# Hybrid decoder block on one core: the first stage with z's first two products in it, norms issued ahead, and other rooms up to the x stage

## The chip, the cores and the metric

The kernel runs on one core of one Trainium2 chip. The metric is the device time of one execution in microseconds; the median of three runs is given. Everything is float32 outside the matmuls; a float32 product is made of three matmuls of rounded parts (high x high, high x low, low x high).

## The reference

One decoder layer over x of 1024 tokens by 1024. Only its first lines matter here:

```python
h = rms_norm(x, g_pre_mix[l])
q, k, v, z, xbc, dt_raw, ga, gs = _split(h @ w_in[l], IN_SIZES)
o_att = stick_breaking_attention(q, k, v)          # heads split and joined
o_ssm = ssd_branch(z, xbc, dt_raw, ...)            # uses silu(z)
merged = sigmoid(ga) * (o_att @ w_br_att[l]) + sigmoid(gs) * (o_ssm @ w_br_ssm[l])
x = x + rms_norm(merged @ w_mix_out[l], g_post_mix[l])
...                                                # cross-attention, SwiGLU
```

q, k and v are 1024 wide each, z 2048, x|B|C 3072, dt 32, the two gates 1024 each.

## The kernel before

The work is a list of instructions for five engines (TensorE, VectorE or DVE, ScalarE or ACT, GpSimd or POOL, and SyncE or SP, whose one queue issues every transfer). Python code writes them in one order. A scheduler then places them by a model of their times: each engine takes, of what the model finds ready, what the code wrote first. On the chip every engine, and SP's queue, runs its own list strictly in order, and waits are semaphores. Memory is cut into pools; a pool is opened and closed with the code block that owns it, on the left or the right end of each partition's memory, and a tile waits for the readers of what lay in its place.

**Strassen-Winograd.** The wide projections of h are made as 2 x 2 block products with seven products in place of eight. h transposed is cut into quarters: b11 and b21 (features 0 to 511 and 512 to 1023 of tokens 0 to 511) and b12, b22 (the same of tokens 512 to 1023), and the combinations t1 = b12 - b11, t2 = b22 - t1, t3 = b22 - b12, t4 = b21 - t2. Each is kept as a rounded part and a residue (`b11h`, `b11l`, ...).

**First stage (the first `with ExitStack() as p1`, pools from `t4x0` on).** `load_x` brings 128 tokens into a tile. `normed(c)` squares it on ACT with a running sum (L332), takes 1/sqrt on POOL (`rstd_of`, L163 and L164) and scales on DVE (L333). `turned` transposes it on TensorE, four 128 x 128 blocks to a PSUM bank (L339). `put` writes rounded part (ACT, L344) and residue (L345). `first_half(c)` for c = 0 to 3 does this for b11 and b21 and also copies both whole to the tiles x11 and x21 (ACT, L365). `second_half(c)` does b12 (rounded by L93, residue by L96 on POOL, both stored to `hb_d`), b22, and the four combinations, t1 from x11 (L380) and t4 from x21 (L384). `dt_raw` makes the 32 columns of dt, 24 small matmuls for each group of tokens (L99 to L101). v's first two products, `a11` x b11 and `a12` x b21, run beside this: `product` gives four steps; a step rounds a 128 x 512 piece of weights (`zh`, ACT, L93), takes its residue (`zl`, DVE, L96) and makes 12 matmuls of 128 x 512 (L287 to L289) into four PSUM banks.

**Second stage (pools `zraw2`, `zk`, `zo`, `zw2`).** `token_major(j, ...)` does a 1024-column block of v (j = 0) or z (j = 1, 2). Its weight blocks b11_, b21_, b22_, b12_ are 1 MB each, in two tiles `zr` of four (`zraw`) and six (`zraw2`) rooms. Products in order: b11 (with a copy u of it), t2, b21, t1, t3, b22, t4, the first and third already done for j = 0. The sums of weights s1, s3, s2 (L468, L470, L472; DVE for j = 0, else POOL) and s4 (L480, POOL) come between. `put_v` and `put_z` (sigmoid on ACT, L432, product on DVE, L433) evacuate and store (L439, L434).

**x stage.** `winograd_weights` loads two tiles `wr` (L191), makes four sums `sf` on POOL (L194 to L197) and rounds seven weights into `sw`; `winograd_pair` runs the seven products (L218 to L220). Conv and gates follow, then attention, the state-space mixer, the output projections, cross-attention and the feed-forward, which uses `winograd_weights` too.

Of the kernel before, what the change touches and what calls it, by code (L numbers as in the profile page):

```python
# [8 lines left out]
F32 = mybir.dt.float32  # L9
# [25 lines left out]
def hybrid_block(ctx, tc, a, out, dbg=None):  # L35
# [20 lines left out]
    def scr(name, shape, dt=F32):  # L56
        return dram.tile(shape, dt, tag=name, name=name)
# [20 lines left out]
    x2_d = scr("x2_d", [S, D])  # L78
    x3_d = scr("x3_d", [S, D])


# [40 lines left out]

    def columns(pp, tag):

        with tc.tile_pool(name="prm", bufs=1) as prp:
            prm = [mk(prp, [P, P], F32, f"prm{i}") for i in range(2)]
            for t in prm:
                G.memset(t, 0.0)
            nc.sync.dma_start(prm[0][0:96, :], a["conv_w"][0].rearrange("t (f p) -> (t f) p", p=P))
            for nm, n in (("conv_b", 24), ("g_ssm_norm", 16)):  # L130
                nc.sync.dma_start(prm[1][rows[nm]:rows[nm] + n, :], a[nm][0].rearrange("(f p) -> f p", p=P))
            for i, t in enumerate(prm):
                ps = mk(pp, [P, 4, P], F32, tag)[:, 0]
                T.transpose(ps, t, ident)
                A.activation(prmT[:, i * P:(i + 1) * P], ps, AF.Copy)
        nc.sync.dma_start(dsk, a["d_skip"][0].partition_broadcast(P))
# [48 lines left out]
    def winograd_weights(rawp, sfp, swp, loads, pool_ops=0):  # L185

        r0 = mk(rawp, [P, 4, 2, P], F32, "wr")
        r1 = mk(rawp, [P, 4, 2, P], F32, "wr")
        for r, kh in ((r0, 0), (r1, 1)):
            for dst, s in loads(r, kh):  # L190
                nc.sync.dma_start(dst, s)  # L191
# [57 lines left out]
    with ExitStack() as pa:  # L249
# [51 lines left out]
        with ExitStack() as p1:  # L301
            t4 = pool(p1, "t4x0", 4)
            sv = pool(p1, "xsv")
            tt = pool(p1, "tcomb", 6)
            bt = pool(p1, "b12t", 1)
            mp = pool(p1, "memp")
# [4 lines left out]
            def load_x(c):  # L311
                xts[c] = mk(t4, [P, D], F32, "x4")
                nc.sync.dma_start(xts[c], x_in[c * P:(c + 1) * P, :])

            load_x(0)
            gx = load_gain(mp, "g_pre_mix")
            load_x(1)
# [7 lines left out]

            x11, x21 = [mk(sv, [P, 4, HALF], F32, n) for n in ("x11", "x21")]

            def normed(c):
                xt = xts[c]
                junk = mk(tt, [P, D], BF16, "tc")  # L330
                ms = mk(stats, [P, 1], F32, "ms")
                A.activation(junk, xt, AF.Square, scale=D ** -0.5, accum_out=ms)  # L332
                V.scalar_tensor_tensor(xt, xt, rstd_of(ms), gx, ALU.mult, ALU.mult)  # L333
                return xt

# [22 lines left out]
            def first_half(c):  # L358
                cs = slice(c * P, (c + 1) * P)
                y = normed(c)  # L360
                q = []
                for kh, (nm, whole_) in enumerate((("b11", x11), ("b21", x21))):
                    pt = turned(y, kh)
                    q.append(put(nm, c, pt))
                    A.activation(whole_[:, :, cs], pt, AF.Copy)  # L365
                return lambda: dt_raw(c, q)

            def second_half(c):

                cs = slice(c * P, (c + 1) * P)  # L370
                y = normed(c + 4)
                x12, x22 = turned(y, 0), turned(y, 1)
# [8 lines left out]
                V.tensor_tensor(t3, x22, t3, ALU.subtract)  # L381
                q22 = put("b22", c, x22)
                V.tensor_tensor(t2, x22, t1, ALU.subtract)
                V.tensor_tensor(t4_, x21[:, :, cs], t2, ALU.subtract)  # L384
                put("t2", c, t2, V)
                put("t1", c, t1, G)
# [4 lines left out]
            a11, a12 = None, None  # L391
            dts_ = []
            for c in range(4):
                dts_.append(first_half(c))
                if c == 0:
                    a11 = block(rv, 0, C_V)
                load_x(c + 4)
                if c == 1:
                    columns(psp, "tr")
                    a12 = block(rv, 512, C_V)  # L400
                if c > 0:
                    dts_.pop(0)()
            pa0 = [mk(psa, [P, HALF], F32, "ma") for _ in range(4)]
            steps = product(pa0, a11, "b11", True, False) + product(pa0, a12, "b21", False, True)
            for c in range(4):
                dts_.append(second_half(c))
                for _ in range(2):
                    steps.pop(0)()
                dts_.pop(0)()
                if c == 1:  # L410
                    u0 = copied(pa0)
            dts_.pop(0)()


        with ExitStack() as p1:
            rp = pool(p1, "zraw2", 6)
            kp = pool(p1, "zk", 6)
            op = pool(p1, "zo", 2)
            wps.append(pool(p1, "zw2", 3))
# [20 lines left out]

            def token_major(j, c0, put, i0):
                bb = ((psa, "ma"), (psb, "mb"))[::1 if j % 2 == 0 else -1]
# [18 lines left out]
                if j == 0:  # L461
                    pa_, u = pa0, u0
                else:
                    pa_ = bank(0)
                    times(pa_, b11_, "b11", True, False)
                s1 = [mk(rp, [P, 2, HALF], F32, "zr") for _ in range(2)]
                E_ = V if j == 0 else G
# [4 lines left out]
                both(lambda q: E_.tensor_tensor(s2[q], s1[q], b11_[q], ALU.subtract))  # L472
                if j > 0:
                    u = copied(pa_)
                pb_ = bank(1)
                times(pb_, s2, "t2", True, True)
                if j > 0:
                    times(pa_, b12_, "b21", False, True)
# [5 lines left out]
                times(pb_, s1, "t1", True, False)  # L484
                for c in range(4):
                    put(c, i0, pa_[c])
                pa_ = bank(0)
# [17 lines left out]

            token_major(0, C_V, put_v, 0)
            token_major(1, C_Z, put_z, 0)
            token_major(2, C_Z + 2 * HALF, put_z, 2)
# [964 lines left out]
    with ExitStack() as q4:  # L1473
        sfp = pool(q4, "fsf", 4, side="right")
        swp = pool(q4, "fsw", 7, side="right")
# [285 lines left out]
```

## Time and profile before

| | |
|---|---|
| median of 3 runs | 2646.32 us (2643.34 to 2647.19) |
| profiled execution | span 2654.0 us |
| TensorE matmul busy | 2519.6 us, 95% of the span |
| DVE busy | 1827.7 us, 69% |
| ACT busy | 1158.9 us, 44% |
| POOL busy | 874.8 us, 33% |
| HBM read, written | 192.37 MB, 68.82 MB |

The profiled execution is one run of its own, and its span is what the rows of the trace add up to; the runs are timed without the profiler. A busy TensorE is not TensorE at its peak, since its clock is gated. A line such as `tr<-ident,x` reads: tile tr is written, from tiles ident and x. In brackets stands how long the engine had been idle before, and what released it.

### The profile page before, as it was taken

How to read it: one execution, taken by the hardware profiler on the slowest of the kernel's cores; microseconds unless marked ns; L12 is line 12 of the kernel's file. 1: busy time of each engine (PE TensorE's matmuls, PEld its weight loads, DVE VectorE, ACT ScalarE, POOL GpSimd, SP SyncE). 2: the span in 40 equal slices, each digit the busy share in tenths (PEclk: the TensorE clock that was granted, in tenths of full speed). 3: DMA queues.
4: the chain of work that ended last, by engine and by line, in shares of the span. 5: the costliest groups of instructions: out<-in, count | busy, mean ns of one | idle time of the engine just before them, and what ended most of it. 6: DMA issues, size and time to landing. Idle time of an engine off the chain costs nothing. (4 is left out here: it accounts for less than half of the span.)

```text
span 2654.0 us, 32762 instructions
## 1 busy us (share of the span) xinstructions
PE 2519.6 (95%) x12090; PEld 2085.9 (79%) x12090; DVE 1827.7 (69%) x2118; ACT 1158.9 (44%) x2061; POOL 874.8 (33%) x684
## 2 busy tenths in 40 slices
PE   6799999999999999989999999999999999999997
PEld 5588787788777778868888878888787888887786
DVE  5547678776589898686688754414549566666997
ACT  5333355555466666465544411314333333334333
POOL 4223444353211121163465231100213333323763
PEclk8799999999999999999999999999999999999999
DMA  4431343333422222246423362321231222223223
GB/s 132 135 107 68 112 127 98 106 96 120 135 65 67 72 76 64 80 145 191 123 81 93 99 210 77 111 88 40 88 123 61 87 82 85 80 87 151 95 105 133
DMA packets 240427, 271.73 MB, mean 102 GB/s; under 512 B 14719, under 2 KB 171016, under 8 KB 239882
## 3 DMA queue, kind: packets, MB, share of 16 engines
q1 hardware_dynamic: 240266, 269.63, 31.9%
q8 instruction: 95, 1.56, 0.2%
q14 instruction: 66, 0.54, 0.1%
HBM read 192.37 MB, written 68.82 MB: 98 GB/s over the span
## 5 line engine op out<-in xcount | busy, mean ns | idle before, releaser
L784 DVE TENSOR_TENSOR_SCAN n<-n,mask 128x128 f32<-128x128 f32 (+7 forms) x128 | 184.3, 1463 | 12.2 <-ACT n L783 11.3
L96 DVE TENSOR_TENSOR sw<-sf,sw 128x512 fp32r<-128x512 f32 x150 | 133.4, 901 | 67.4 <-ACT sw L93 67.0
L194 POOL TENSOR_TENSOR sf<-wr,wr 128x512 f32<-128x512 f32 x38 | 57.5, 1513 | 286.2 <-DMA wr<-in_w_in_dram 109.7
L803 ACT ACTIVATE wth<-tr,mone 128x512 fp32r<-128x512 f32 x192 | 111.1, 581 | 78.7 <-PE tr L800 77.0
L93 ACT ACTIVATE sw<-sf 128x512 fp32r<-128x512 f32 x150 | 92.0, 626 | 112.4 <-PE mm L220 95.9
L93 ACT ACTIVATE sw<-wr 128x512 fp32r<-128x512 f32 x113 | 71.0, 629 | 133.5 <-PE mm L220 126.8
L804 DVE SCALAR_TENSOR_TENSOR wtl<-tr,wth 128x512 fp32r<-128x512 f32 x192 | 101.5, 546 | 39.4 <-ACT wth L803 38.0
L220 PE MATMUL mm<-h,sw 128*128 128x512 f32 x320 | 124.8, 391 | 1.8 <-DVE sw L96 1.8
L99 PE MATMUL mm<-oth,bw 128*128 128x512 f32 (+1 forms) x320 | 122.2, 382 | 4.1 <-ACT a L1080 1.7
L218 PE MATMUL mm<-h,sw 128*128 128x512 f32 x320 | 122.6, 391 | 2.9 <-ACT h L93 2.3
L219 PE MATMUL mm<-h,sw 128*128 128x512 f32 x320 | 125.1, 391 | 0.0
L96 DVE TENSOR_TENSOR sw<-wr,sw 128x512 fp32r<-128x512 f32 x113 | 103.4, 916 | 27.8 <-ACT sw L93 19.9
L101 PE MATMUL mm<-oth,bw 128*128 128x512 f32 (+1 forms) x320 | 119.5, 373 | 0.9 <-DVE bw L96 0.9
L100 PE MATMUL mm<-otl,bw 128*128 128x512 f32 (+1 forms) x320 | 118.8, 371 | 0.0
L552 DVE SCALAR_TENSOR_TENSOR b<-b,prmT,b 128x1023 f32<-128x1023 f32 (+2 forms) x72 | 106.1, 1473 | 14.1 <-ACT b L550 13.4
L89 POOL TENSOR_SCALAR v<-va 128x512 fp32r<-128x512 f32 x16 | 20.1, 1260 | 288.4 <-PE av L813 148.2
L96 DVE TENSOR_TENSOR zl<-zr,zh 128x512 fp32r<-128x512 f32 x84 | 72.4, 870 | 56.7 <-ACT zh L93 56.5
L783 ACT ACTIVATE n<-sc 128x512 f32<-128x512 f32 (+1 forms) x192 | 89.2, 486 | 49.8 <-PE sc L782 25.8
L163 POOL TENSOR_SCALAR rstd<-ms 128x1 f32<-128x1 f32 x82 | 30.4, 371 | 242.8 <-ACT x L1302 114.5
L99 PE MATMUL p<-bw,h 128*128 128x512 f32 x256 | 99.4, 394 | 3.3 <-DVE x L1304 2.4
L93 ACT ACTIVATE zh<-zr 128x512 fp32r<-128x512 f32 x84 | 52.2, 630 | 112.5 <-PE mb L289 58.4
L101 PE MATMUL p<-bw,h 128*128 128x512 f32 x256 | 100.6, 394 | 0.0
(600 smaller groups left out, 8276.7 us busy)
## 6 DMA issues: line engine op xcount, KB each, us to landing
wr<-in_w_gu_dram SPq DMA_DIRECT2D x80, 256.0 KB
wr<-in_w_in_dram SPq DMA_DIRECT2D x36, 512.0 KB
zr<-in_w_in_dram SPq DMA_DIRECT2D x24, 512.0 KB
gu_d<-t SPq DMA_DIRECT2D x44, 256.0 KB
wraw<-in_w_in_dram SPq DMA_DIRECT2D x20, 512.0 KB
x<-in_x_dram SPq DMA_DIRECT2D x16, 512.0 KB
zs_d<-zo SPq DMA_DIRECT2D x32, 256.0 KB
xs_d<-b SPq DMA_DIRECT2D x32, 256.0 KB
```

Of the source, the lines that this page charges most:

```text
L93: A.activation(o, i, AF.Copy)
L96: eng.tensor_tensor(o, i, hi.bitcast(F32), ALU.subtract)
L99: first = T.matmul(ps, sh, mh, start=start, stop=False)
L100: T.matmul(ps, sh, ml, start=False, stop=False)
L101: T.matmul(ps, sl, mh, start=False, stop=stop)
L218: T.matmul(ps, w[0][:, k, :], b[0][:, k, :], start=first and k == 0, stop=False, skip_group_check=True)
L219: T.matmul(ps, w[0][:, k, :], b[1][:, k, :], start=False, stop=False, skip_group_check=True)
L220: T.matmul(ps, w[1][:, k, :], b[0][:, k, :], start=False, stop=last and k == 3, skip_group_check=True)
L552: V.scalar_tensor_tensor(acc[:, sh:], y[:, :S - sh], cw(3 - sh, f), acc[:, sh:], ALU.mult, ALU.add)
L784: V.tensor_tensor_scan(nt[:, 0:L][:, ::-1], nt[:, 0:L][:, ::-1], mask[:, S - L:][:, ::-1], 1.0, ALU.mult, ALU.max)
L803: A.activation(wh[:, t0 * P:], pt[:, t0 * P:], AF.Identity, bias=mone)
L804: V.scalar_tensor_tensor(wl[:, t0 * P:], pt[:, t0 * P:], -1.0, wh[:, t0 * P:].bitcast(F32), ALU.add, ALU.subtract)
```

## The change

z's first two products (columns 3072 to 3583, times b11 and b21) are made in the first stage behind v's, in the same four banks. `ahead` gives for v and for z a load and eight steps; after step 3 the first product is kept, v's as u in SBUF (`u_kept`), z's through a small tile to memory (`u_away`, `u_d`), and after step 7 the first output block is evacuated and stored (`v_out`, `z_out`). The 16 steps go between the second halves, three to one.

`normed` is called one to two groups ahead of the half that uses it, and its square's output has a tile of its own. x11 and x21 are gone: t1 and t4 are made from the rounded part and residue of b11 and b21, two subtractions each instead of one, so that eight copies on ACT go and eight subtractions on DVE come.

Rooms: `zraw2` is opened before the first stage, on the right, and also holds the rows of x, the gain and the square's output; `zraw` and `zw` go to the left, `zk` and `zo` to the right. v's first-half weights are loaded a second time in the second stage, since z's have taken their tiles. `token_major` skips the two products for j = 0 and now also for j = 1, whose u is loaded back from `u_d`. In the x stage the rounded weights `xsw` go to the left, and the fourth sum gets a pool of its own (`xsf4`); the feed-forward's sums are split in the same way.

```diff
-    def columns(pp, tag):
+    def columns(pp, tag, sp, stag):
...
-        s1, s2, s3, s4 = [mk(sfp, [P, 4, P], F32, "sf") for _ in range(4)]
+        s1, s2, s3, s4 = [mk(pl, [P, 4, P], F32, "sf") for pl in (sfp[0], sfp[0], sfp[0], sfp[1])]
...
-        rv = pool(pz, "zraw", 4, side="right")
-        wv = pool(pz, "zw", 3, side="right")
+        rp = pool(pz, "zraw2", 6, side="right")
         zu = pool(pz, "zu", 4, side="right")
+        rv = pool(pz, "zraw", 4)
+        wv = pool(pz, "zw", 3)
...
-            t4 = pool(p1, "t4x0", 4)
-            sv = pool(p1, "xsv")
             tt = pool(p1, "tcomb", 6)
+            ep = pool(p1, "early", 4)
...
-                    A.activation(whole_[:, :, cs], pt, AF.Copy)
...
-                V.tensor_tensor(t1, x12, x11[:, :, cs], ALU.subtract)
+                V.tensor_tensor(t1, x12, b11[0], ALU.subtract)
+                V.tensor_tensor(t1, t1, b11[1], ALU.subtract)
...
-                V.tensor_tensor(t4_, x21[:, :, cs], t2, ALU.subtract)
+                V.tensor_tensor(t4_, b21[0], t2, ALU.subtract)
+                V.tensor_tensor(t4_, t4_, b21[1], ALU.add)
...
+            def u_away(ps):
+                for c in range(4):
+                    t = mk(ep, [P, HALF], F32, "early")
+                    A.activation(t, ps[c], AF.Copy)
+                    nc.sync.dma_start(u_d[c], t)
...
+            load_v, steps_v = ahead(C_V, v_out, u_kept)
+            load_z, steps_z = ahead(C_Z, z_out, u_away)
+            normed(0)
+            normed(1)
             dts_ = []
             for c in range(4):
                 dts_.append(first_half(c))
+                load_x(c + 4)
                 if c == 0:
-                    a11 = block(rv, 0, C_V)
-                load_x(c + 4)
+                    load_v()
+                if c < 2:
+                    normed(c + 2)
...
-            for c in range(4):
-                dts_.append(second_half(c))
-                for _ in range(2):
-                    steps.pop(0)()
-                dts_.pop(0)()
-                if c == 1:
-                    u0 = copied(pa0)
-            dts_.pop(0)()
+            normed(4)
+            for i, s in enumerate(steps_v + steps_z):
+                if i == 4:
+                    load_z()
+                if i % 3 == 0 and i < 12:
+                    c = i // 3
+                    dts_.append(second_half(c))
+                    if c < 3:
+                        normed(c + 5)
+                if dts_ and i % 3 == 1:
+                    dts_.pop(0)()
+                s()
+            for d in dts_:
+                d()
...
-            kp = pool(p1, "zk", 6)
-            op = pool(p1, "zo", 2)
+            kp = pool(p1, "zk", 6, side="right")
+            op = pool(p1, "zo", 2, side="right")
...
-                if j == 0:
-                    b11_, b12_ = a11, a12
-                    b21_, b22_ = block(rp, 0, c0 + HALF), block(rp, 512, c0 + HALF)
-                else:
+                if not early:
...
+                    b21_, b22_, b11_, b12_ = block(rp, 0, c0 + HALF), block(rp, 512, c0 + HALF), block(rv, 0, c0), block(rv, 512, c0)
+                    u = us[j]
+                    if u is None:
+                        u = [mk(zu, [P, HALF], F32, "zu") for _ in range(4)]
+                        for c in range(4):
+                            nc.sync.dma_start(u[c], u_d[c])
...
-            sfp = pool(p1, "xsf", 4, side="right")
-            swp = pool(p1, "xsw", 9, side="right")
+            sfp = pool(p1, "xsf", 3, side="right"), pool(p1, "xsf4", 1, side="right")
+            swp = pool(p1, "xsw", 9)
```

More of the change, by code (lines that the diff above doesn't have):

```diff
@@ L79, in hybrid_block @@
     x3_d = scr("x3_d", [S, D])
+    u_d = scr("u_d", [4, P, HALF])
     turn = [0]
@@ L121, in hybrid_block @@
     prmT = mk(cp, [P, 256], F32, "prmT")
-    def columns(pp, tag):
[L125 to L135, printed above, removed]
+    def columns(pp, tag, sp, stag):
+        both = mk(sp, [P, 4, P], F32, stag)
+        prm = [both[:, i] for i in range(2)]
+        G.memset(both[:, 0:2], 0.0)
+        nc.sync.dma_start(prm[0][0:96, :], a["conv_w"][0].rearrange("t (f p) -> (t f) p", p=P))
+        for nm, n in (("conv_b", 24), ("g_ssm_norm", 16)):
+            nc.sync.dma_start(prm[1][rows[nm]:rows[nm] + n, :], a[nm][0].rearrange("(f p) -> f p", p=P))
+        for i, t in enumerate(prm):
+            ps = mk(pp, [P, 4, P], F32, tag)[:, 0]
+            T.transpose(ps, t, ident)
+            A.activation(prmT[:, i * P:(i + 1) * P], ps, AF.Copy)
         nc.sync.dma_start(dsk, a["d_skip"][0].partition_broadcast(P))
@@ L324, in hybrid_block @@
             lo_of(wdl, wd, wdh, G)
-            x11, x21 = [mk(sv, [P, 4, HALF], F32, n) for n in ("x11", "x21")]
             def normed(c):
                 xt = xts[c]
-                junk = mk(tt, [P, D], BF16, "tc")
+                junk = junks[:, (c % 2) * HALF:(c % 2 + 1) * HALF].bitcast(BF16)
                 ms = mk(stats, [P, 1], F32, "ms")
@@ L358, in first_half @@
             def first_half(c):
-                cs = slice(c * P, (c + 1) * P)
-                y = normed(c)
                 q = []
[L362 to L365, printed above, removed]
+                for kh, nm in enumerate(("b11", "b21")):
+                    q.append(put(nm, c, turned(xts[c], kh)))
                 return lambda: dt_raw(c, q)
@@ L389, in second_half, with v_out, z_out, u_kept @@
                 return lambda: dt_raw(c + 4, (q12, q22))
-            a11, a12 = None, None
+            def v_out(c, i, x, to):
+                A.activation(to, x, AF.Copy)
+                nc.sync.dma_start(v_d[1 + c * P:1 + (c + 1) * P, i * HALF:(i + 1) * HALF], to)
+            def z_out(c, i, x, to):
+                A.activation(to, x, AF.Sigmoid)
+                V.tensor_tensor(to, x, to, ALU.mult)
+                nc.sync.dma_start(zs_d[c * P:(c + 1) * P, i * HALF:(i + 1) * HALF], to)
+            def u_kept(ps):
+                return copied(ps)
+            def u_away(ps):
[3 more added lines that the diff above has]
+                    nc.sync.dma_start(u_d[c], t)
+            us = []
+            def ahead(c0, out_, keep):
+                st = {}
+                def load():
+                    st["w"] = block(rv, 0, c0), block(rv, 512, c0)
+                def open_():
+                    st["ps"] = [mk(psa, [P, HALF], F32, "ma") for _ in range(4)]
+                    st["s"] = product(st["ps"], st["w"][0], "b11", True, False) + product(st["ps"], st["w"][1], "b21", False, True)
+                def step(i):
+                    def run():
+                        if i == 0:
+                            open_()
+                        st["s"][i]()
+                        if i == 3:
+                            us.append(keep(st["ps"]))
+                        if i == 7:
+                            for c in range(4):
+                                out_(c, 0, st["ps"][c], mk(ep, [P, HALF], F32, "early"))
+                    return run
+                return load, [step(i) for i in range(8)]
+            load_v, steps_v = ahead(C_V, v_out, u_kept)
+            load_z, steps_z = ahead(C_Z, z_out, u_away)
+            normed(0)
+            normed(1)
             dts_ = []
@@ L439, in put_v, with token_major @@
                 nc.sync.dma_start(v_d[1 + c * P:1 + (c + 1) * P, i * HALF:(i + 1) * HALF], vt)
-            def token_major(j, c0, put, i0):
+            def token_major(j, c0, put, i0, early=False):
                 bb = ((psa, "ma"), (psb, "mb"))[::1 if j % 2 == 0 else -1]
@@ L472, in token_major @@
                 both(lambda q: E_.tensor_tensor(s2[q], s1[q], b11_[q], ALU.subtract))
-                if j > 0:
+                if not early:
                     u = copied(pa_)
@@ L476, in token_major @@
                 times(pb_, s2, "t2", True, True)
-                if j > 0:
+                if not early:
                     times(pa_, b12_, "b21", False, True)
@@ L484, in token_major @@
                 times(pb_, s1, "t1", True, False)
-                for c in range(4):
-                    put(c, i0, pa_[c])
+                if not early:
+                    for c in range(4):
+                        put(c, i0, pa_[c])
                 pa_ = bank(0)
```

32 lines of the change are left out of this document (14 added, 18 removed).

## The prediction

> **What bounds the kernel now.** I read the page's first line, then the stretches of the first 311 us, then the waits of TensorE, then the timeline of each engine where TensorE stands still.
>
> ```profile
> span 2654.0 us, 32762 instructions
> ```
>
> The stretches (us; busy time of TensorE, its weight loads, DVE, ACT and POOL; granted clock, DMA share, GB/s):
>
> ```profile
> 8.02:49.38 41.36, 39.79 (x290) 34.09 (x290) 26.22 (x33) 29.23 (x60) 17.05 (x19) 1.00 0.45 152
> 49.38:86.45 37.07, 10.62 (x64) 8.21 (x64) 19.33 (x21) 14.00 (x28) 13.94 (x15) 0.53 0.37 115
> 86.45:95.78 9.33, 8.16 (x18) 5.95 (x19) 9.23 (x8) 3.29 (x6) 5.40 (x2) 0.50 0.19 56
> 95.78:298.59 202.81, 202.81 (x895) 167.60 (x893) 115.96 (x159) 73.45 (x120) 41.34 (x17) 1.00 0.30 99
> 298.59:305.14 6.55, 0.00 (x1) 0.00 (x1) 6.02 (x6) 1.74 (x4) 6.47 (x6) 0.91 0.32 122
> 305.14:311.04 5.90, 5.90 (x14) 4.64 (x15) 5.69 (x5) 2.37 (x5) 5.90 (x5) 0.52 0.12 44
> ```
>
> The reader is to see four things. From 8 to 49 us TensorE is full: transposes, dt products and all eight steps of v's first two products. From 49.38 to 86.45 it works 10.62 of 37.07 us, at half clock, and no engine is full: a chain of latencies. From 95.78 to 298.59 it is 100% busy, so a matmul taken out there is time. Then 6.55 us idle ahead of the x stage, with a slow clock behind it. Who was waited for in the first 520 us (us in all, times, longest):
>
> ```profile
> PE tr L339 <- DVE x L333: 16.4, 3, 8.0
> PE mb L287 <- ACT zh L93: 14.0, 1, 14.0
> ```
>
> The first row is the norms (8.0 of it the start-up), the second the end of the stage, where the weights come late.
>
> **z's first two products move.** The TensorE rows that price them, from its timeline (start, duration):
>
> ```profile
> 8.02 1.97 PE L339 MATMUL tr<-ident,x 128*128 128x128 f32 x8 [8.02 <-DVE x L333]
> ...
> 34.42 0.22 PE L99 MATMUL pdt<-b12h,wdh 128*32 128x128 f32 x1
> ...
> 35.80 0.22 PE L101 MATMUL pdt<-b22h,wdl 128*32 128x128 f32 x1
> ...
> 42.31 1.04 PE L339 MATMUL tr<-ident,x 128*128 128x128 f32 x8
> ...
> 99.18 0.39 PE L287 MATMUL mb<-zh,t2h 128*128 128x512 f32 x1
> ...
> 102.36 0.39 PE L289 MATMUL mb<-zh,t2l 128*128 128x512 f32 x1
> ```
>
> From 99.18 to 102.36 there are 15 starts: 3.18/14 = 0.227 us a matmul. Two products are 8 steps of 12, 96 matmuls, 21.8 us. They leave the full stretch behind 95.78: **gain 21.8**. There 17 products of 48 stay, 816 x 0.227 = 185.3 us.
>
> They are paid for only as far as they don't fit into the idle of 49 to 86. TensorE's list for the new first stage: 16 steps x 12 x 0.227 = 43.6; eight dt products of 24, with 23 gaps in 35.80 - 34.42 = 1.38, so 1.44 each, 11.5; eight groups of eight transposes at 1.04, 8.3. In all 63.4, from 8.02, and some 2 more since the first two groups take 1.97 at the cold clock: ready at 73.4 if it never waits.
>
> DVE is the other candidate. Its rows: a weight residue beside a POOL subtraction, a subtraction with an operand in PSUM, one with both in SBUF, the norm's scaling; then the mean residue of 27 to 49.4 us, and the stretch up to 86.45.
>
> ```profile
> 38.79 1.78 DVE L96 TENSOR_TENSOR zl<-zr,zh 128x512 fp32r<-128x512 f32 x1
> ...
> 59.27 0.68 DVE L383 TENSOR_TENSOR tc<-tr,tc 128x512 f32<-128x512 f32 x1
> 59.98 1.07 DVE L384 TENSOR_TENSOR tc<-x,tc 128x512 f32<-128x512 f32 x1
> ...
> 62.65 2.27 DVE L333 SCALAR_TENSOR_TENSOR x<-x,rstd,g_pre_mix 128x1024 f32<-128x1024 f32 x1 [0.99 <-POOL rstd L164]
> ```
>
> ```profile
> L96 DVE TENSOR_TENSOR zl<-zr,zh 128x512 fp32r<-128x512 f32 x5 | 5.6, 1142 | 1.9 <-ACT zh L93 1.9
> ```
>
> ```profile
> 0.00:86.45 86.45, 50.41 (x354) 42.31 (x354) 46.84 (x53) 46.18 (x91) 32.84 (x46) 0.80 0.45 144
> ```
>
> DVE has 46.84 now. Added: 8 residues of z at 1.14, 9.1; 8 subtractions for the copies that are gone (t1 and t4 each take b's high and low part one after the other) at 1.07, 8.6; z's gating, 4 x 0.68, 2.7. Sum 67.2, and its first work starts some 7 us in: 74, as late as TensorE's 73.4. Two engines nearly full in a chain wait for each other; from 8.02 to 49.38 TensorE lost 1.6 us with DVE 63% busy, and here DVE is about 90% busy, so I add 6.5 and take **80 us** for the end of the stage; bounds 74 (no waits) and 91.7 (below). The transposes are no longer held by the norms, whose square, rstd and scaling now run one half ahead, with a room of their own for the square's output. If that cover goes, two second halves stand as far apart as today,
>
> ```profile
> 53.44 1.94 PE L339 MATMUL tr<-ident,x 128*128 128x128 f32 x8 [4.10 <-DVE x L333]
> ...
> 65.07 1.94 PE L339 MATMUL tr<-ident,x 128*128 128x128 f32 x8 [4.28 <-DVE x L333]
> ```
>
> 11.6 us, which three steps of z (8.2) with transposes and dt product (2.5) nearly fill.
>
> ACT and POOL stay hidden. ACT loses eight copies of x and gains eight roundings, z's eight evacuations:
>
> ```profile
> L365 ACT ACTIVATE x<-tr 128x512 f32<-128x512 f32 x7 | 4.2, 594 | 2.1 <-DVE b11l L345 1.1 <-DVE b21l L345 1.0
> ```
>
> That is 8 x 0.59 = 4.8 less and 16 x about 0.6 = 9.6 more, on 46.18 of 86.45: 51 of 80. POOL's subtractions are the same ones.
>
> Today the stage's real cost is 86.45 plus what the slow clock and a wait cost behind it: 18 matmuls in 9.33 us, against 18 x 0.227 = 4.1, so 5.2 more: 91.7. **Gain 91.7 - 80 = 11.7** (0 to 17.7). It asks that v's second-half weights are there at 80. They come late today, since their room is opened only behind the first stage:
>
> ```profile
> 73.91 0.93 SPq L268 DMA_DIRECT2D zr<-in_w_in_dram  x2
> ```
>
> ```profile
> 80.98 1.23 DVE L468 TENSOR_TENSOR zr<-zr,zr 128x1024 f32<-128x1024 f32 x1 [7.70 <-DMA zr<-in_w_in_dram]
> ```
>
> 7.1 us from issue to use. With the six rooms open from the start, shared with x's rows, a tile can follow as soon as x's fifth to eighth rows are transposed, well ahead of 73.
>
> **Queues.** SP gets four stores and four loads of z's u (256 KB each) and four loads of v's first-half weights a second time, since z takes their tiles: 2 + 2 MB. At the 152 GB/s of the first stretch that is some 27 us of transfer, beside a DMA share under 0.5; the 54.5 us of v's five remaining products hide it. What stands in SP behind a store that waits for its evacuation waits with it; that is the third rival. z's first step needs v's four banks, and so v's four copies: under one 0.59 copy of wait for the first, the rest runs ahead of the matmuls.
>
> **z's second block starts with another product.** Its sums s1, s3, s2 on POOL had a first-half product in front of them as cover. The trace shows that they are done in time without it; the last s2 and v's last sum:
>
> ```profile
> 142.37 2.39 POOL L472 TENSOR_TENSOR zr<-zr,zr 128x1024 f32<-128x1024 f32 x1 [2.02 <-DVE zl L96]
> ```
>
> ```profile
> 144.26 0.69 DVE L503 TENSOR_TENSOR zu<-zu,ma 128x512 f32<-128x512 f32 x1 [2.04 <-PE ma L289]
> ```
>
> The last s2 ends at 144.76, where v's last sums begin, and it is wanted two steps into the product. But that product writes the banks which those sums read, and u comes back by a load that can start only when v's u has been copied out: four sums of 0.69, a copy of 0.59, 7.1 for the load (as from 73.91 to 80.98), one sum, 11.1 against the 10.9 of the product that hides it. I take a **loss of 2**, bounds 0 and 7 (the load takes twice as long).
>
> **The x stage's rooms.**
>
> ```profile
> 291.21 1.56 SPq L191 DMA_DIRECT2D wr<-in_w_in_dram  x3
> ```
>
> ```profile
> 304.03 1.05 POOL L89 TENSOR_SCALAR sw<-wr 128x512 fp32r<-128x512 f32 x1
> ```
>
> Today the loads go out at 291.21, 7.4 ahead of the idle time; POOL then works until 304.03 on four sums before it rounds the first weight. The raw weights move over z's raw tiles, which DVE read last at 283.03:
>
> ```profile
> 283.03 0.69 DVE L96 TENSOR_TENSOR zl<-zr,zh 128x512 fp32r<-128x512 f32 x1 [1.51 <-ACT zh L93]
> ```
>
> So the loads can go 7 to 8 us earlier, and only the fourth sum waits for the last z rows. The rounded weights lie over z's rounded ones, free when the last product has read them. I take 1.5 us of idle instead of 6.55, and no cold clock (14 matmuls in 5.90 against 3.2: 2.7): **gain 7.8**, bounds 1.7 (only the fourth sum leaves POOL's way) and 9.3. The split of the feed-forward's sum room changes no order that I can see: 0, within a few us either way, as for all that comes later.
>
> **Sum**: 21.8 + 11.7 + 7.8 - 2 = 39.3. The profiled 2654.0 becomes 2614.7; the runs' median of 2646.32 lies 7.7 below that span, so 2646.3 - 39.3 = **2607.0**.
>
> **A rule against it.** POOL's residue of t4 beside the 1.78 us row of DVE:
>
> ```profile
> 38.19 1.84 POOL L345 TENSOR_TENSOR t4l<-tc,t4h 128x512 fp32r<-128x512 f32 x1 [0.64 <-ACT t4h L344]
> ```
>
> DVE's op ends at 40.57, 0.54 behind POOL's end at 40.03: it stood still until POOL was through. The Trainium skill, page "SBUF — State Buffer", section "SBUF: two separate sides", says that a DVE op with two SBUF inputs and a GpSimd op exclude each other for the whole instruction; this row agrees. By that page the price of the 16 added ops hangs on how often the two engines meet: at each of the 16, it is the first rival's.
>
> **Rivals.** *DVE becomes the bound.* All 16 added all-SBUF ops meet a POOL op and take 1.78: 28.5 instead of 17.7, 10.8 more. DVE's list is then 78, from 7 on, 85, and with the same share of waits 92.6. For it: the residue's mean of 1.14; against it: POOL is busy 17.05 of 41.36, so that most ops meet none. Time 2607 + 12.6 = 2620.
>
> *z's products don't reach the gaps*: their raw tiles wait for v's, and behind stores in SP. Then they follow the last dt product, which ends the stage's work on TensorE today at 86.45 - 14.0 = 72.4, and t2 starts at 72.4 + 21.8 = 94.2: 2607 + 14 = 2621. Against it: v's first raw tile is free once its second step is rounded, long before 49 us.
>
> *Loads behind stores, at each block's start.* SP is one queue; v's and z's early stores now stand in it between the weight loads, and each waits for an evacuation. Late weights at a block's start have a price in this trace: 14.0 of waiting and 5.2 of cold clock, 19.2. At the three block starts (v's rest, z's first, z's second) that is 57.6: 2607 + 58 = 2665, slower. At two, 38.4: 2645, no change. It decides from 13 us at each of three. Against it: behind 95.78 the same queue, with the same kind of stores in it, let TensorE run 202.81 of 202.81.
>
> **How the numbers follow.** The forecast 0.66, its own range 2595 (stage end 74, no losses: 48.8 gained, and a few us from later stages) to 2628 (stage end 90, x stage 1.7, z's start -7: 18.2). DVE 0.13, late z 0.10: both near 2620. Loads at two starts 0.05, at three 0.06. Range 2595 to 2632, which leaves out the last two and the tails. A measurement of this kernel tells apart about 0.2%, 5.3 us: faster 0.89, within 0.05, slower 0.06.
>
> **What would show it.** Right: in the new trace the eight z steps stand between second halves; TensorE has no wait of over 4 us for the norm; its first t2 matmul starts at 74 to 90; from there to the x stage's first matmul about 189 us; no cold clock there. Wrong: TensorE idle over 10 us ahead of t2 with DVE released by a DMA (third rival), DVE over 95% busy from 20 us to t2 (first), z matmuls behind the last dt product (second), or a 5 us wait for s2 or u at z's first block.

## The result, and the profile after

| | before | changed |
|---|---|---|
| median of the first comparison (4 runs each) | 2646.1 us | 2619.6 us |
| lowest to highest | 2643.3 to 2647.2 | 2616.4 to 2621.9 |
| ratio, 95% interval | | 0.990 [0.989, 0.992] |
| profiled span | 2654.0 | 2620.1 |

The change saves 26.5 us, 1.0%. Forecast were 39.3 us and 2607.0, with 2595 to 2632 as the range. The direction and the places were right; 12.6 us of the gain are missing.

First the stretches of the changed kernel, cut where those of before were cut: up to t2's first matmul, its last part, from there to the x stage's first matmul, and the 20 us behind that (columns: length; busy time of TensorE, weight loads, DVE, ACT, POOL; granted clock, DMA share, GB/s).

```profile
span 2620.1 us, 32774 instructions
```

```profile
0.00:84.44 84.44, 68.41 (x451) 56.01 (x451) 68.34 (x75) 49.89 (x99) 41.61 (x45) 1.00 0.65 208
40.00:84.44 44.44, 38.79 (x234) 30.99 (x232) 43.46 (x47) 25.51 (x50) 25.56 (x15) 1.00 0.51 156
84.44:269.77 185.33, 185.25 (x817) 153.08 (x816) 115.80 (x151) 65.52 (x110) 48.93 (x21) 1.00 0.35 118
269.77:289.77 20.00, 17.76 (x74) 13.30 (x73) 18.74 (x17) 8.69 (x16) 14.26 (x10) 1.00 0.44 132
```

The latency chain at half clock (10.62 busy of 37.07 us) is gone: the first stage now holds 451 matmuls where it held 354, at full clock. The second row shows what came in its place: DVE works 43.46 of 44.44 us. The third row is the full stretch, 202.81 before and 185.33 now, without a gap. The fourth shows 2.2 us of idle time in the first 20 us of the x stage. The TensorE waits of the first 520 us and the two marks, from its timeline:

```profile
PE tr L338 <- DVE zr L333: 7.8, 1, 7.8
PE ma L289 <- DVE zl L97: 4.3, 4, 1.5
...
PE pdt L101 <- DVE b22l L344: 2.2, 3, 1.2
...
PE mm L220 <- DVE sw L97: 1.4, 1, 1.4
```

```profile
84.44 1.07 PE L288 MATMUL mb<-zh,t2h 128*128 128x512 f32 x4
...
269.77 0.39 PE L218 MATMUL mm<-b11h,sw 128*128 128x512 f32 x1
...
272.72 0.50 PE L220 MATMUL mm<-b11h,sw 128*128 128x512 f32 x1 [0.77 <-POOL sw L97]
...
276.64 0.50 PE L220 MATMUL mm<-b21h,sw 128*128 128x512 f32 x1 [1.38 <-DVE sw L97]
```

Of the 16.4 us of norm waits only the start-up's 7.8 is left, and the 14.0 for late weights are gone. t2 starts at 84.44, the x stage at 269.77 instead of 305.14: **35.4 us earlier. The runs show 26.5.** So two questions stand: why t2 starts at 84.4 and not at 80, and where 9 us went behind 270 us.

### The profile page after: what moved, and what is told of

Its sections match the earlier page's. It is cut to its first block, busy times and chain, and to the rows that moved or that the text cites. A ratio compares the mean times of both kernels' runs of the same rounds, so it can differ in the third digit from the quotient of the medians.

```text
span 2620.1 us, 32774 instructions
## 1 busy us (share of the span) xinstructions
PE 2509.6 (96%) x12090; PEld 2077.3 (79%) x12090; DVE 1834.0 (70%) x2126; ACT 1152.3 (44%) x2053; POOL 887.9 (34%) x683
## 5 line engine op out<-in xcount | busy, mean ns | idle before, releaser
L97 DVE TENSOR_TENSOR sw<-sf,sw 128x512 fp32r<-128x512 f32 x150 | 127.8, 865 | 63.9 <-ACT sw L94 63.5
L97 DVE TENSOR_TENSOR sw<-wr,sw 128x512 fp32r<-128x512 f32 x113 | 106.3, 943 | 29.6 <-ACT sw L94 25.3
L97 DVE TENSOR_TENSOR zl<-zr,zh 128x512 fp32r<-128x512 f32 x84 | 72.6, 878 | 40.6 <-ACT zh L94 40.5
L196 POOL TENSOR_TENSOR sf<-wr 128x512 f32<-128x512 f32 x38 | 63.6, 1672 | 107.3 <-DVE sw L97 107.3
```

The lines of the kernel that those rows point to most:

```text
L97: eng.tensor_tensor(o, i, hi.bitcast(F32), ALU.subtract)
```

## The experiments

### 1. The kernel before, again

No edit. My first theory was that the profile of before had been an unusually long execution; the rival, that the changed kernel's had.

> The kernel before, unchanged, profiled a second time. The two traces differ by 33.9 us (2654.0 to 2620.1), the runs by 26.5 (2646.1 to 2619.6). First theory: the first profile of the kernel before caught an execution that was some 8 us slow; a new one spans 2644 to 2648, and the 8 us are found in one place of the old trace. Rival: the profile of this kernel is always that long (2652 to 2656), and the profile itself costs it 8 us that the changed kernel does not pay.

Measured: 2645.95 us median (10 runs), ratio 0.9995 [0.998, 1.001]. The span of its profile is 2639.6, 14.4 under the first one, and the x stage starts at 304.7 (305.1). So the first 305 us are the same in both, and the difference lies behind them: 2.6 us in the x stage, 2.8 between it and attention, 8 in attention (first to last score matmul 396.7 instead of 404.6). So the first profile was indeed a long execution. But the new span lies below the expected 2644 to 2648, and the difference stands in several places and not in one.

### 2. Eight DVE operations fewer

```diff
                 V.tensor_tensor(t1, x12, b11[0], ALU.subtract)
-                V.tensor_tensor(t1, t1, b11[1], ALU.subtract)
 ...
                 V.tensor_tensor(t4_, b21[0], t2, ALU.subtract)
-                V.tensor_tensor(t4_, t4_, b21[1], ALU.add)
```

> The changed kernel without the second subtraction for t1 and the addition for t4 (b11's and b21's residues are left out of the two combinations): eight DVE operations less, which took 3.7 and 6.9 us. First theory, DVE is what bounds the new first stage (it stands still under 1.5 us from 37 to 84): the first t2 matmul moves from 84.4 to 75 to 78, the time falls by 6 to 9 us against the changed kernel, ratio to the kernel before about 0.987. Rival, the stage is bound by the arrival of x and of the weights (DMA share about 0.8 in the first 40 us) and DVE only follows: t2 within 1.5 us of 84.4, ratio 0.990.

Measured: 2621.45 us (2616.6 to 2625.0), ratio 0.990 [0.988, 0.992]; t2 at 84.77. DVE's busy time up to t2 fell by 6.0 us and t2 did not move. The eight operations were 10.6 us; in their place the 21 weight residues took longer (18.8 us before this edit, see the rivals below):

```profile
L97 DVE TENSOR_TENSOR zl<-zr,zh 128x512 fp32r<-128x512 f32 x21 | 23.3, 1137 | 1.0 <-ACT zh L94 1.0
```

Its stretches:

```profile
0.00:84.80 84.80, 70.72 (x451) 58.58 (x452) 62.34 (x67) 51.83 (x101) 38.39 (x45) 0.98 0.63 207
...
30.00:40.00 10.00, 6.96 (x60) 5.56 (x58) 9.11 (x9) 6.82 (x17) 6.01 (x5) 1.00 0.89 303
40.00:50.00 10.00, 9.70 (x48) 8.29 (x49) 7.01 (x11) 6.78 (x14) 5.24 (x4) 0.83 0.37 124
50.00:70.00 20.00, 20.00 (x133) 16.65 (x132) 18.48 (x18) 11.37 (x23) 11.92 (x7) 1.00 0.51 148
```

My theory that DVE alone sets the end fell. TensorE waited less in all, but in another place: it lost 3 us of its 10 between 30 and 40 us, most of it at these two matmuls of a dt product. That product stands in front of a step of v in this kernel's compiled order and behind it in the changed kernel's (the compiled order is the one in which the scheduler, called the planner from here on, has placed the instructions of each engine):

```profile
38.05 0.25 PE L100 MATMUL pdt<-b22h,wdh 128*32 128x128 f32 x1 [0.68 <-ACT b22h L343]
40.30 0.29 PE L101 MATMUL pdt<-b22l,wdh 128*32 128x128 f32 x1 [2.00 <-DVE b22l L344]
```

A slow clock followed (0.83, 48 matmuls in 9.70 us), then 20 us without any gap. With DVE lighter, the waits moved to another place and the end stayed. That TensorE is then the bound is likely for 50 to 70 us and not shown for the whole stage. In this experiment, and in 3, 7, 8 and 9, the planner also wrote another order of the first stage, so that each shows its edit and a new order together.

### 3. z's two products back in the second stage

```diff
-            for i, s in enumerate(steps_v + steps_z):
-                if i == 4:
-                    load_z()
-                if i % 3 == 0 and i < 12:
-                    c = i // 3
+            for i, s in enumerate(steps_v):
+                if i % 2 == 0:
+                    c = i // 2
 ...
-            token_major(1, C_Z, put_z, 0, True)
+            token_major(1, C_Z, put_z, 0)
```

> The changed kernel, but z's first two products made in the second stage again, as before; norms ahead, no copies, and rooms as changed. First theory (DVE-bound first stage, z's eight steps fit only in part): the first stage loses z's residues (8 x 0.92 = 7.4 us of DVE) and t2 starts near 77; then 19 products of 10.9 follow, and the x stage starts near 77 + 207 = 284, 14 us later than with the change; ratio about 0.996. Rival (TensorE-bound first stage): t2 starts 21.8 earlier, near 63, the x stage at the same 270, ratio 0.990. Second rival (z's products fit whole, at no cost): t2 stays at 84 and the x stage starts at 291, ratio 0.998.

Measured: 2632.54 us (2630.1 to 2633.9), ratio 0.994 [0.993, 0.996].

```profile
0.00:80.50 80.50, 49.68 (x354) 40.24 (x355) 64.39 (x65) 42.22 (x83) 40.78 (x44) 0.86 0.55 181
...
80.50:288.30 207.80, 207.80 (x915) 172.05 (x914) 119.76 (x161) 75.81 (x126) 47.72 (x22) 1.00 0.30 99
```

The full stretch grows by 207.80 - 185.33 = 22.5, and t2 comes only 3.9 earlier. By this run z's 96 matmuls thus cost the first stage 3.9 us, and the move is worth 18.5 at the x stage's start (288.3 against 269.8). None of the three expected marks was met. Without z, t2 starts at 80.5 and TensorE runs on without a gap, where before it started its next stretch at 86.45 and waited again: that part comes from the rooms and the earlier loads and norms alone.

### 4. The x stage's rooms as before

```diff
-            sfp = pool(p1, "xsf", 3, side="right"), pool(p1, "xsf4", 1, side="right")
-            swp = pool(p1, "xsw", 9)
+            sfp = (pool(p1, "xsf", 4, side="right"),) * 2
+            swp = pool(p1, "xsw", 9, side="right")
```

> The changed kernel with the x stage's rooms as before: four sums in one pool, rounded weights on the right. First theory: TensorE stands still for 5 to 7 us ahead of the x stage's first matmul and has a cold clock for 5 us behind it; 7 to 10 us slower than the changed kernel, ratio about 0.993. Rival: with z's raw rooms elsewhere the loads come early anyway, the idle time stays under 2 us, ratio 0.990.

Measured: 2628.44 us (2624.8 to 2633.4), ratio 0.993 [0.991, 0.994].

```profile
277.83 0.79 PE L218 MATMUL mm<-b11h,sw 128*128 128x512 f32 x1 [7.54 <-POOL sw L90]
```

```profile
277.80:284.00 6.20, 6.17 (x16) 4.88 (x17) 4.29 (x3) 1.72 (x4) 6.20 (x6) 0.57 0.15 26
```

The wait for the first rounded weight is back (7.54), and so is the slow clock behind it (0.57). The x stage starts 8.0 later, as the first theory has it. The time grew by less than its 7 to 10: the gain over the kernel before is 20.2 us here against 26.5, so some 6 us are lost. The first stage's compiled order is the changed kernel's, instruction by instruction.

### 5 and 6. The changed kernel again, and with the norms not ahead in the text

> The changed kernel, unaltered, timed again with a new profile. Open is why its first 305 us show 35.3 us gained (x stage's first matmul at 269.8 against 305.1) and the medians only 26.5. Theory 1 (nothing later has changed; the four executions of it so far lay high by chance of the attention's rhythm): the median comes to 2611 to 2616, 32 to 36 us under that of the kernel before. Theory 2 (the stages behind the x stage's start run some 6 us longer after the change): the median stays at 2617 to 2622, 25 to 30 us under, while t2 starts at 84 to 85.5 and the x stage at 269 to 271 again.

Measured: 2618.02 us (2613.8 to 2619.7), ratio 0.990 [0.988, 0.991]; t2 at 84.52, the x stage at 269.88. 26.6 us under the kernel before: the second theory's range. The first theory, chance, fell.

```diff
             def first_half(c):
+                normed(c)
 ...
             def second_half(c):
 ...
+                normed(c + 4)
 ...
-            normed(0)
-            normed(1)
 ...
-                if c < 2:
-                    normed(c + 2)
 ...
-            normed(4)
 ...
-                    if c < 3:
-                        normed(c + 5)
```

> The changed kernel with each norm again inside the half that it belongs to, instead of one half ahead. Theory 1 (the norms ahead are what keeps TensorE supplied between second halves): the waits of TensorE for the norm of about 4 us before each of the four second halves return, v's and z's steps cannot pass them, t2 starts at 90 to 98 and the time is 6 to 13 us longer. Rival (v's and z's steps in TensorE's list cover the norm chain, since the stage is paced by DVE and TensorE together): no norm wait of over 2 us, t2 within 2 us of 84.4, the time the same within 3 us.

Measured: 2615.61 us (2614.3 to 2620.3), ratio 0.989 [0.988, 0.991]; t2 at 84.29, no norm wait but the start-up's. The median is 29.1 us under the kernel before, still short of the first theory's 32 to 36 of experiment 5. The rival's numbers, for a simpler reason: the planner sets the order itself, and the compiled lists of all engines are the same, instruction by instruction, as the changed kernel's. The place of the norms in the text did nothing, and this run is a third sample of the changed kernel.

### 7. t4's second operation on POOL

```diff
-                V.tensor_tensor(t4_, t4_, b21[1], ALU.add)
+                G.tensor_tensor(t4_, t4_, b21[1], ALU.add)
```

> The changed kernel with the second operation of each t4 (b21's low part added, 4 in all, 6.9 us on DVE at a mean of 1723 ns) on POOL instead of DVE. POOL has 41.6 us of work before t2 and DVE 68.3. Theory 1 (from 40 us on DVE, 99% busy, sets the pace): DVE is 7 us lighter, t2 starts at 78 to 82, the time 2 to 6 us shorter. Rival (the latency chain from one half to the next and TensorE's own list set it, as leaving out eight such operations suggested): t2 at 84 to 86, the time the same within 2 us. Third (POOL's longer operations stretch more of DVE's two-operand operations, t4's chain gets longer): t2 at 86 to 90, the time 2 to 6 us longer.

Measured: 2620.52 us (2618.3 to 2623.8), ratio 0.991 [0.989, 0.992]; t2 at 87.31, the x stage at 272.6. t2 comes 2.9 later, as the third theory has it, and its mechanism shows: DVE's busy time up to t2 is 67.34 instead of 68.34 though 6.9 us were taken off it, since the same 21 residues took 21.5 instead of 18.8. The time differs from the changed kernel's by less than the runs scatter.

```profile
L97 DVE TENSOR_TENSOR zl<-zr,zh 128x512 fp32r<-128x512 f32 x21 | 21.5, 1048 | 0.1
```

### 8. v's second weight block behind x in SP's queue

```diff
-                    st["w"] = block(rv, 0, c0), block(rv, 512, c0)
+                    st["w"] = block(rv, 0, c0), None
+
+                def load2(mark):
+                    st["w"] = st["w"][0], block(rv, 512, c0, mark)
 ...
+                if c == 1:
+                    load_v[1](xld[5])
```

> The changed kernel with the two loads of v's second weight block (1 MB) put in SP's queue behind the load of x's sixth row block instead of ahead of its fifth. Theory 1 (in the first 30 us the arrival of x sets the pace: ACT waits 11.0 us for x's row blocks while DMA moves 255 to 277 GB/s, and 1 MB at that rate is 3.8 us): the second halves' transposes begin 2 to 4 us earlier, t2 at 80.5 to 82.5, the time 2 to 4 us shorter. Rival (DVE and TensorE, both nearly full from 30 us on, eat that lead, or v's second block comes late for its steps): t2 at 84 to 86, the time the same within 2 us.

Measured: 2616.37 us (2612.8 to 2617.4), ratio 0.989 [0.987, 0.990]; t2 at 85.61, in the rival's range. But the edit hardly moved what it was meant to move. DVE's scaling of x's last two row blocks:

```profile
28.88 1.28 DVE L336 SCALAR_TENSOR_TENSOR zr<-zr,rstd,zr 128x1024 f32<-128x1024 f32 x1 [3.00 <-POOL rstd L164]
30.93 2.31 DVE L336 SCALAR_TENSOR_TENSOR zr<-zr,rstd,zr 128x1024 f32<-128x1024 f32 x1 [0.16 <-POOL rstd L164]
```

In the changed kernel these stand at 29.36 and 31.41, so they came 0.5 us earlier and not the 2 to 4 of the first theory. Whether an earlier arrival of x would bring t2 forward stays open.

### 9. The squares in the sums' rooms

```diff
-                junk = junks[:, (c % 2) * HALF:(c % 2 + 1) * HALF].bitcast(BF16)
+                junk = junks[:, (c % 2) * HALF:(c % 2 + 1) * HALF].bitcast(BF16) if c < 4 else mk(tt, [P, D], BF16, "tc")
```

> The changed kernel with one room changed: the squares of x's rows five to eight are written into the rooms of the second half's sums (six, as in the kernel before) instead of a room of their own; the norms stay issued ahead in the text. Theory 1 (it is the square's own room that lets the norms run ahead; the place in the text does nothing, as putting them back in place moved t2 by 0.1 us): x's last row block is scaled at 50 to 65 us instead of 31.4, TensorE waits 4 us for the norm before two or three of the second halves, t2 starts at 90 to 98 and the time is 6 to 14 us longer. Rival (v's and z's steps cover the norms however late they come): t2 at 84 to 87, the time the same within 3 us.

Measured: 2616.53 us (2613.6 to 2620.5), ratio 0.988 [0.987, 0.990]. DVE's scaling of the last four row blocks, and then the stretch up to t2:

```profile
21.40 1.29 DVE L333 SCALAR_TENSOR_TENSOR zr<-zr,rstd,zr 128x1024 f32<-128x1024 f32 x1 [2.54 <-POOL rstd L164]
37.98 1.27 DVE L333 SCALAR_TENSOR_TENSOR zr<-zr,rstd,zr 128x1024 f32<-128x1024 f32 x1
53.31 1.27 DVE L333 SCALAR_TENSOR_TENSOR zr<-zr,rstd,zr 128x1024 f32<-128x1024 f32 x1
67.51 1.28 DVE L333 SCALAR_TENSOR_TENSOR zr<-zr,rstd,zr 128x1024 f32<-128x1024 f32 x1
```

```profile
0.00:91.17 91.17, 68.48 (x451) 57.07 (x451) 70.03 (x77) 52.12 (x100) 40.27 (x44) 0.95 0.64 206
```

The norms run late again, at 38, 53 and 68 us, much as in the kernel before (37.59, 51.02 and 62.65), instead of 24.46, 29.36 and 31.41 in the changed kernel. t2 starts at 91.17, 6.7 later, and the x stage at 278.9. The square's room is what lets the norms run ahead. The mechanism is the first theory's; but TensorE's waits are at the dt products (5.6 for b22's high part, 4.9 for its low part), not at the transposes. And the time did not grow: the 9 us were made up later, most of them in one stage. From its first state product to its last output product the SSM stage took 1498.3 - 1111.2 = 387.1, where the three profiles of the changed kernel have 394.2 to 395.9:

```profile
L100 PE MATMUL mm<-oth,bw x320: 280/389/500, 1143.4 to 1498.3; 128*128 128x512 f32 x128, 128*128 128x256 f32 x32
...
L100 PE MATMUL pst<-s2r,bh x28: 389/389/794, 1111.2 to 1436.6; 128*128 128x512 f32 x28
```

Nothing in that stage's text was touched. Its compiled order differs: the planner's lists, which depend on the whole program, were written anew.

### 10 to 12. The kernel before, three more profiles

> The kernel before, unaltered, for one more profile of its later stages. From the x stage's first matmul to the end the medians of the runs give some 2340 us for it and some 2347 for the changed kernel, while its two profiles gave 2348.9 and 2334.9. Theory 1 (the attention stage runs longer after the change): attention from its first to its last score matmul 395 to 400 us here, against 399 to 404 in eight profiles of changed kernels. Theory 2 (no difference; each profile draws its own rhythm): 398 to 405, and the span 2640 to 2655.

> The kernel before, unaltered, a third time for the same question: theory 1 attention 395 to 400 us, theory 2 398 to 405.

> The kernel before, unaltered, a fourth time for the same question: theory 1 attention 395 to 400 us, theory 2 398 to 405.

Measured: spans 2640.6, 2641.3 and 2642.8; attention 399.9, 398.1 and 399.6 us. With the two earlier profiles of before, and the three of the changed kernel, the means (and ranges) of five marks are:

| mark (us) | before, 5 profiles | changed, 3 profiles | difference |
|---|---|---|---|
| x stage's first matmul | 304.4 (303.5 to 305.1) | 269.8 (269.6 to 269.9) | 34.6 |
| first score matmul | 707.4 (705.5 to 711.7) | 674.5 (672.5 to 676.4) | 32.9 |
| last score matmul | 1107.2 (1102.6 to 1116.3) | 1077.6 (1075.4 to 1080.5) | 29.6 |
| SSM's last output product | 1527.5 (1523.2 to 1537.3) | 1499.7 (1497.0 to 1503.5) | 27.8 |
| end | 2643.7 (2639.6 to 2654.0) | 2615.6 (2612.0 to 2620.1) | 28.1 |

The 34.6 us shrink step by step to 28, and that is what the runs show (26 to 29 over the comparisons). What is known of each step:

*x stage up to the first score, 1.7.* Its first 20 us, in the third profile of before (experiment 10) and the second of the changed kernel (experiment 5):

```profile
303.50:323.50 20.00, 19.97 (x79) 16.31 (x80) 14.10 (x14) 8.11 (x16) 14.64 (x11) 0.89 0.33 96
```

```profile
269.90:289.90 20.00, 17.75 (x73) 13.11 (x72) 18.93 (x17) 8.67 (x16) 14.26 (x10) 1.00 0.43 132
```

Before, the stage starts late and slowly (clock 0.89) but then runs through; now it starts early and waits 2.15 us for residues of weights, with DVE 18.93 of 20 us busy. By the prediction's 2.7 for the slow clock these two rows alone would make the step some 0.5 us shorter. TensorE's compiled order in this stage differs too, and what makes the step longer stays open.

*Attention, 3.3.* Its compiled order is the same on all engines, so no instruction was moved. The same program takes 396.7 to 404.6 (before) and 400.7 to 404.3 (changed); a long execution shows more waits for the scaled q. In the first profile of before, and in the third:

```profile
PE mm L99 <- DVE qs L727: 6.1, 5, 1.5
PE sc L781 <- DMA kh<-kh: 2.3, 1, 2.3
```

```profile
PE mm L99 <- DVE qs L727: 2.5, 2, 1.4
...
PE sc L781 <- DMA kh<-kh: 0.5, 1, 0.5
```

Over the five profiles of before this wait is 0, 1.1, 2.3, 2.5 and 6.1 us where attention takes 396.7, 398.1, 399.6, 399.9 and 404.6; in the three of the changed kernel it is 2.8, 4.9 and 5.1 at 400.7, 404.1 and 404.3. So the wait goes with the length of the stage, and why it differs between executions of one program stays open. The three new profiles lie in the first theory's range (395 to 400) and in the second's (398 to 405) as well, so they don't decide between the two. One changed kernel, without the x rooms, took 398.8. That attention became longer through the change is possible and not shown.

*SSM, 1.8.* The compiled order differs on all engines, and experiment 9 shows, by one profile, what another order of this stage may do: 7.8 us.

A version with the first stage as changed and the SSM order of experiment 9 would gain some 8 us more by these numbers. It wasn't tried, since the planner writes that order and no line of the text sets it.

## Why the prediction was right or wrong

**z's move, 21.8.** Right: 22.5 us left the full stretch (experiment 3). That its cost falls into the first stage's idle time was right too: 3.9 us of it showed.

**The first stage's end, 80.** 4.4 us short, though within its bounds of 74 and 91.7; the gain is 91.7 - 84.4 = 7.3 instead of 11.7. Against the working: start at 7.79 (8.02 taken), TensorE's list 68.41 (65.4), other waits 8.24 (6.5). So the list was sized 3.0 too small and the waits 1.7. Of the 8.24, 4.3 are waits for DVE's weight residues. DVE's list came out nearly as sized, 68.34 against 67.2. Where a wait comes from, 75 to 80 us:

```profile
76.04 2.50 POOL L529 TENSOR_TENSOR zr<-zr,zr 128x1024 f32<-128x1024 f32 x1 [3.77 <-DVE t2l L344]
76.21 2.88 DVE L382 TENSOR_TENSOR tc<-tc,b21l 128x512 f32<-128x512 f32 x1
79.02 0.68 DVE L97 TENSOR_TENSOR zl<-zr,zh 128x512 fp32r<-128x512 f32 x1
...
79.75 0.50 PE L289 MATMUL ma<-zl,b21h 128*128 128x512 f32 x1 [1.05 <-DVE zl L97]
```

A 0.68 us operation with two SBUF operands takes 2.88 beside POOL's sum and ends 0.55 behind it. z's residue stands behind it, and TensorE behind the residue. The POOL sum is v's own s4: with the weights early, the sums of v's second block moved in among the second halves (DVE's first at 47.91 instead of 80.98), which I had not followed up. The row bears out the rule of the Trainium skill that the prediction named ("SBUF — State Buffer", "SBUF: two separate sides").

**The norms.** Right that they run ahead and that TensorE no longer waits for them, and right about the room; wrong to count the place in the text as part of the cause (experiments 6 and 9). "If that cover goes" named the right dependence and sized it too small: z's steps were to fill 10.7 of each 11.6 us, 0.9 left over, and t2 came 6.7 later in experiment 9, with the waits at the dt products.

**z's block start, -2.** The loss was 0: 185.33 us from t2 to the x stage, all but 0.08 busy, against 185.3 for the matmuls alone.

**The x stage's rooms, 7.8.** At the stage's start 6.55 us of idle and the slow clock went, as worked out (experiment 4: 8.0 at that mark). But new waits of 2.15 us follow at once, since the residues of the weights, made by POOL and DVE (L97), are not there yet. I asked what is late next for the first rounded weight alone.

**"0, within a few us either way, as for all that comes later."** This step failed. By its terms up to the x stage's first matmul (21.8 + 11.7 + 5.05 of idle - 2) the forecast was 36.6, and 34.6 came. That these are close is in part luck: in the first profiles the stage's end gave 4.4 less than forecast, while z's block start and the x stage's idle time gave 2.0 and 1.5 more. The slow clock's 2.7 was to bring 39.3 at the first score, and 32.9 was measured. Then attention and SSM took 5 back. The span of 2654.0 that carried the sum was also the longest of five profiles (the others 2639.6 to 2642.8); subtracting 7.7 for it was right for the level.

**The rivals.** *DVE becomes the bound*: its sign, over 95% busy from 20 us to t2, did not appear as stated (58.91 of 64.44 us, 91%), though from 40 us on DVE was 97.8% busy:

```profile
20.00:84.44 64.44, 58.03 (x386) 47.36 (x384) 58.91 (x64) 39.37 (x81) 34.45 (x26) 1.00 0.59 187
```

Its price did not appear either. The stage ended at 84.4, not 92.6, and lightening DVE by 6 us moved nothing (experiment 2): its condition, that all 16 added operations meet a POOL operation, didn't hold. Their groups up to t2 (busy us, mean ns; the first holds all 21 weight residues, z's eight among them):

```profile
L97 DVE TENSOR_TENSOR zl<-zr,zh 128x512 fp32r<-128x512 f32 x21 | 18.8, 921 | 0.6 <-ACT zh L94 0.6
...
L382 DVE TENSOR_TENSOR tc<-tc,b21l 128x512 f32<-128x512 f32 x4 | 6.9, 1723 | 0.1
...
L371 DVE TENSOR_TENSOR tc<-tc,b11l 128x512 f32<-128x512 f32 x4 | 3.7, 936 | 0.0
```

Of the three groups only t4's second operations met one in most cases: three of the four took 1.66 to 2.88 us, the fourth 0.67. The 16 come to 8 x 0.92 + 6.9 + 3.7 = 18.0, and 17.7 was taken.

*z's products don't reach the gaps*: most of them did. In TensorE's order 69 of z's 96 matmuls stand ahead of the last dt product and 27 behind it, which was this rival's sign; t2 still came at 84.4, not at its 94.2. Only nine stand ahead of the last transposes (55.3 us), so that z's steps run between the dt products rather than between the second halves, as the prediction's first sign had it. *Loads behind stores at block starts*: none; no wait for a weight load stands at any of the three.

## What to carry to other kernels

Idle time of TensorE ahead of a full stretch can be filled with matmuls out of that stretch at a small part of their price (3.9 of 22.5 us here), but once a second engine is nearly full beside it, neither engine's list alone sets the end, and taking work off one of them need not move it. What an instruction waits for is its room and its data, not its line: where a planner orders the program, look at which buffer holds it back. And a planner may write the order of an untouched stage anew: a gain of some 10 us is to be followed mark by mark to the end over several profiles before it is believed.

## What the runs showed that was not expected

The same program, profiled five times, ran its attention stage in 396.7 to 404.6 us, though its instructions stand in the same order each time. In one profile, another compiled order of an unedited SSM stage was worth 7.8 us (387.1 against a mean of 394.9), as much as the whole of the x stage's rooms. And in experiment 2 TensorE's granted clock was 0.83 from 40 to 50 us, right behind two waits of 0.68 and 2.00 us with a single matmul between them. The Trainium skill, page "TensorE: Matmul & The Clock Gate", Part 1, puts the fall at one idle window of about 3.4 us; by these two waits, 2.68 us in all, somewhat less is enough.
